# Hyena transform tables: split once, kept in a slab of their own for both layers

## Chip, cores and metric

One core of one Trainium2 chip runs the whole program in one launch. The metric is the time of an execution on the device in microseconds (us), the median over several runs; lower is better.

## What is computed

The reference is one step of a model with two layers over two streams of tokens, 128 of a prompt and 256 of a sample, 384 together, each token 1024 wide and in float32. A layer normalises, runs three token mixers on one projection, merges them by gates, and ends in a convolutional feed-forward part:

```python
h = rms_norm(x, lp["norm1"]) * (1 + sc1) + sh1
proj = h @ lp["w_in"]
q_a, k_a, v_a, cq, ckv, kpe, hy_in, gates = jnp.split(proj, _split_points(), axis=-1)
...
o_c = hyena_branch(hy_in, lp)
...
x = x + g1 * o
h = rms_norm(x, lp["norm2"]) * (1 + sc2) + sh2
x = x + g2 * conv_ffn(h, lp)
```

The third mixer, Hyena, filters 512 channels twice with long convolutions:

```python
u = dwconv3(hy_in, lp["hy_short_w"], lp["hy_short_b"])
v, x1, x2 = jnp.split(u, 3, axis=-1)
z = v
for n, gate in enumerate((x1, x2)):
    z = gate * (long_conv(z, kf[:, n]) + lp["hy_bias"][n] * z)
```

where `long_conv` is a product of Fourier transforms. The kernel does these transforms as matmuls with cosine and sine tables.

## The kernel before

Everything is feature-major: x lies in SBUF as 8 tiles of 128 features by 384 tokens. Products are kept at float32 accuracy by splitting both sides into a rounded part (hi) and the rest (lo) and adding three one-pass matmuls, hi by hi (line 267), hi by lo (line 268) and lo by hi (line 269), in `mm3`. A split is `hi_lo`: ScalarE rounds a copy (`copy_a`, line 229) and VectorE subtracts (line 233). Weights come by DMA from the queue of SyncE (SP) into a ring of two places (`load_w`, line 247; the modulation weights by line 368), are split, and wait in four pairs of places.

A layer begins with `norm_h`: a sum of squares by matmul (line 421), its root (line 403), a broadcast by matmul (line 427), and then for each of the 8 tiles a product on VectorE (line 236 through `tt`), scale and shift on ScalarE (line 435, two instructions for the two streams), and the split into hi and lo, which the even tiles have from VectorE alone (line 442 and line 236) and the odd ones from both engines (lines 229 and 233). The first product of `hyena_in` needs hi of a tile for lines 267 and 269 and lo for line 268. It runs through the 8 tiles for each block of 128 output features; three blocks can be under way, in three banks of PSUM.

The tables of the Hyena transforms are one input of 12 blocks of 128 by 128. `hyena_open`, called once in each layer between the two halves of `hyena_in`, takes memory for both parts from the arena FA, loads the input and splits it; `hyena_close` gives the memory back after the attention projections.

```python
def hyena_open(y):
    y.oT = [RA.alloc(4, T, top=True) for _ in range(2)]
    y.db = [RA.alloc(12, 128, top=True) for _ in range(2)]
    y.dt = [b.ap() for b in y.db]
    st = FA.alloc(12, 128)
    sp.dma_start(out=st.ap(), in_=t_dft.rearrange("p (a b) -> p a b", b=128))
    hi_lo(y.dt[0], y.dt[1], st.ap())
    st.free()
```

Their readers are the `mm3` calls of `hyena_chain`.

The order on each engine is not the order of the text: the framework schedules the whole program by a simulated time, so an instruction can stand far ahead of its place in the text once its inputs are there. In layer 1 the split of the tables, written after half of the projection, stands in the middle of the norm ahead of that projection. The engines take their instructions strictly in the order that was set.

Of the kernel before, what the change touches and what calls it, by code (L numbers as in the profile page):

```python
# [14 lines left out]
D = 1024  # L15
# [24 lines left out]
N_W = 4  # L40
N_BASE = 9728
SLABS = (1408, *[3072] * 9)
R_RE = 0.25
# [6 lines left out]
class Slab:  # L50
    """A place in SBUF, empty or a tile of one type; parts of it are given out."""

# [28 lines left out]
class Arena:  # L81
    """Memory given out by the order of emission: of the places that are free, the one free for longest."""

# [35 lines left out]
class Rounded:  # L119
    """The same memory, for parts that the tensor engine takes in one pass."""  # L120

# [38 lines left out]
class Ring:  # L160
    """Places of one size in turn."""

# [21 lines left out]
def kernel(  # L184
# [15 lines left out]
    split_slab = Slab(ctx, tc, 2 * N_W * 1024, "split")  # L200
    h_slab = Slab(ctx, tc, 2 * KD * T, "h")
    FA = Arena([Slab(ctx, tc, n, f"s{i}") for i, n in enumerate(SLABS)])
    RA = Rounded(FA)

    def banks(**lines):
        """Gives each line of work its banks of PSUM, which it takes in turn."""
        for line, own in lines.items():
            turns[line] = [int(b) for b in own]
# [12 lines left out]
    def ps_pair(line, n):  # L221
        """Two adjacent banks, the two parts of a tile in one each."""
        own = turns[line]
        b = min((b for b in own if b + 1 in own), key=lambda b: max(own.index(b), own.index(b + 1)))
        turns[line] = [q for q in own if q not in (b, b + 1)] + [b, b + 1]
        return all_banks[:, b:b + 2, 0:n]
# [4 lines left out]
    def hi_lo(hi, lo, src):  # L231
        copy_a(hi, src)
        dve.tensor_tensor(out=lo, in0=src, in1=f(hi), op=ALU.subtract)  # L233
# [68 lines left out]

# [1 line left out]
    def add_sq(k, src, first):  # L304
# [18 lines left out]

# [1 line left out]
    V_B, V_N1, V_N2, V_HW, V_HB, V_HF = 0, 48, 56, 64, 100, 112  # L325
# [45 lines left out]
    def mod_vec(l, v, ready=(), bufs=()):  # L371
        """One of the modulation vectors of both conditions; yields after each piece."""
        gv = ps_of("md", 512)
# [27 lines left out]
    def rstd_of(out, squares):  # L401
        """1 / sqrt(mean + eps) of the sums of squares of D elements."""
        act.activation(out=out, in_=squares, func=AF.Sqrt, scale=1.0 / D, bias=eps_t)
        dve.reciprocal(out=out, in_=out)

    def sqrt_ahead(part):
        """Has the activation engine load the function before the sums are complete."""
        b = FA.alloc(1)
        act.activation(out=b.ap(), in_=part, func=AF.Sqrt)
        b.free()  # L410

    def norm_h(l, which):
        """RMSNorm and modulation of x: the two f32r parts of h, feature-major."""
        hi, lo = h_parts
# [31 lines left out]
    def gemm_f(out, w, m):  # L446
        """The product of a block of weights; yields halfway through a long one."""
        kk = w[0].shape[1]
        for k in range(kk):
            mm3(out, at(w, slice(None), k), (m[0][:, k], m[1][:, k]), k == 0, k == kk - 1)  # L450
            if kk > 6 and k == 3:
                yield

    def conv3(l, dst, src, w0, w1, w2, bias):
        """Centred depthwise convolution of width 3 along the tokens of both streams."""
        act.activation(out=dst, in_=src, func=AF.Identity, scale=vec(l, w1), bias=vec(l, bias))  # L456
        for _, a, b in STREAMS:
            stt(dst[:, a + 1:b], src[:, a:b - 1], vec(l, w0), dst[:, a + 1:b], ALU.mult, ALU.add)
            stt(dst[:, a:b - 1], src[:, a + 1:b], vec(l, w2), dst[:, a:b - 1], ALU.mult, ALU.add)

# [1 line left out]
    def reduce_sin(l, dst, src, fr, b, n, np_):  # L462
        """sin(freq * (src + b)), the argument brought into [-pi, pi]."""
        a = FA.alloc(n)
# [14 lines left out]
    def filters(l, R, spec, first=False):  # L479
        """Spectra of the filters of a layer at the frequencies k + 1/2, per order (Re, Im) of the even and of the  # L480
        odd k for the sample's length, and (Re, Im) for the prompt's, each with the bias, a tap at 0; from the sums
        and differences of the two directions, where |f| + |b| = max(|f + b|, |f - b|) and the backward tap at 0 is
        left out; yields after each piece."""
        zt, w1, w2 = FA.alloc(T), FA.alloc(64), FA.alloc(2, 64)
# [173 lines left out]

# [1 line left out]
    C_E, C_O, I_E, I_O, C_P, I_P = 0, 2, 4, 6, 8, 10  # L660
# [4 lines left out]
    def hyena_start(l, spec):  # L665
# [5 lines left out]
        return y, line  # L671

    def hyena_open(y):
        y.oT = [RA.alloc(4, T, top=True) for _ in range(2)]
        y.db = [RA.alloc(12, 128, top=True) for _ in range(2)]
        y.dt = [b.ap() for b in y.db]
        st = FA.alloc(12, 128)
        sp.dma_start(out=st.ap(), in_=t_dft.rearrange("p (a b) -> p a b", b=128))
        hi_lo(y.dt[0], y.dt[1], st.ap())
        st.free()  # L680

    def hyena_close(y):
        for b in y.db:
            b.free()

    def hyena_in(y, hf, hT):
        """Projection and short convolution of half of the channels; token-major, the second half of the
        sample reversed."""
        l = y.l
# [34 lines left out]
    def hyena_chain(y, hf):  # L724
        """Both long convolutions of half of the channels and their gates."""
        R, dt, tok = RA, y.dt, y.tok[hf]
# [78 lines left out]

# [1 line left out]
    def attn_proj(l, hT, proj):  # L807
        """Queries, keys, values and latents, token-major, into (q k, v, cq ckv kpe) of each token tile."""
        col = 0
# [23 lines left out]
    def rope(dst, src, tab, i, heads, rd, tmp):  # L833
        """Rotates interleaved pairs: dst = src * cos + swapped(src) * (-sin, sin)."""
        cs = tab[:, i, 0].unsqueeze(1).to_broadcast([128, heads, rd])
        sn = tab[:, i, 1].rearrange("p (a b) -> p a b", b=2).unsqueeze(1).to_broadcast([128, heads, rd // 2, 2])
        sw = src.rearrange("p h (a b) -> p h a b", b=2)[:, :, :, ::-1]
        tt(tmp.rearrange("p h (a b) -> p h a b", b=2), sw, sn, ALU.mult)
        tt(dst, src, cs, ALU.mult)
        tt(dst, dst, tmp, ALU.add)  # L840

    def prep(l, proj, q, R):
        """Norms and rotations: queries, keys and latents, transposed."""
        gb = FA.alloc(768)
# [93 lines left out]
    def softmax(ps, nh, nk, scale):  # L938
        """Softmax over the last axis of the scores in PSUM."""
        pb = FA.alloc(nh, nk)  # L940
# [18 lines left out]
    def attention(heads, q_of, kp_of, ks_of, vp_of, vs_of, scale, oT, pairs=False):  # L959
        """Attention of a group of heads; the output feature-major."""  # L960
        jobs = []
# [3 lines left out]
        def scores(hs, i, n):  # L965
            """Queries by the one part of the keys, or by their two."""
            if pairs:
# [42 lines left out]
        def prompt_turn(hs, pb):  # L1010
            """Heads in order of parity in the tile."""
            for half in range(2):
# [58 lines left out]
    def mla(l, q, proj, oT, R):  # L1071
# [26 lines left out]
        def turned(qb, dst, sl):  # L1098
            """An even head is (nope, pe, 0) of 128 rows, an odd one (0, pe, nope)."""
            pt = ps_of("at", 4, 128)  # L1100
# [90 lines left out]
    def gates(l, n, hT, ring, out):  # L1191
        """tanh(g / 2) of the gate columns of a branch: sigmoid(g) is half of 1 + that."""
        for q in range(4):
# [12 lines left out]
    def branch(l, n, gs, oT, m, merged):  # L1206
        """Adds 2 * sigmoid(gates) * projection of a branch; the last halves the sum and splits it."""
        for q in range(4):
# [131 lines left out]
    class Ahead:  # L1340
        """Modulation vectors whose weights are loaded ahead, to fill the wait for a norm."""

# [22 lines left out]
    def urgent(line, by):  # L1365
        """The steps of a line, scheduled as if emitted that many instructions earlier."""
        if by < 0:
# [13 lines left out]
    def weave(main, *sides):  # L1381
        """Emits main with steps of the sides, (line, steps for each step of main), in between."""
        credit = [0.0] * len(sides)
# [11 lines left out]
    def mix(*lines):  # L1395
        """Steps of the lines in turn."""
        lines = list(lines)
# [58 lines left out]
    for l in range(NL):  # L1456
# [16 lines left out]
        finish(ch)  # L1473
        hyena_close(y)
        banks(**PS_AT)
# [139 lines left out]
```

## Time and profile before

| what | value |
|---|---|
| median of 3 runs | 1530.9 us (1530.8 to 1531.94) |
| span of the profiled execution, first to last instruction | 1528.9 us |
| median less span: what lies around the span | 2.0 us |
| TensorE busy (PE) | 1484.3 us, 97% |
| VectorE busy (DVE) | 1014.6 us, 66% |
| ScalarE busy (ACT) | 756.9 us, 50% |
| GpSimd busy (POOL) | 91.1 us, 6% |
| mean granted TensorE clock | 0.991 of full speed |

Busy time is the time in which an engine had an instruction under way. The table is to be read from TensorE down: the span holds 44.6 us in which TensorE had nothing under way, and a mean clock below 1 says that part of its busy time ran at the lower of its two clocks. All times below are counted from the first instruction of the span.

### The profile page before, as it was taken

The page shows a single profiled execution, that of the slowest core. Times are in us where ns is not written, and L with a number is a line of the kernel's source. Part 1 is how long each engine was busy: PE and PEld are TensorE (multiplying, and loading weights), DVE is VectorE, ACT ScalarE, POOL GpSimd, SP SyncE. Part 2 cuts the span into 40 slices and gives each one's busy share as a digit, 9 for nine tenths or more (in the row PEclk, how much of TensorE's full clock was granted, in tenths as well). Part 3 has the DMA queues.
Part 4 walks back from the last instruction along what each step waited for, and adds up shares of the span by engine and source line. Part 5 has one row for each costly group of instructions (what it writes and reads, how often), then busy time and mean ns, then how long its engine had stood idle before and what let it go on. Part 6 is the DMA issues. An engine that isn't in the chain of part 4 may idle for free.

```text
span 1528.9 us, 22323 instructions
## 1 busy us (share of the span) xinstructions
PE 1484.3 (97%) x8615; PEld 1349.2 (88%) x8615; DVE 1014.6 (66%) x1946; ACT 756.9 (50%) x1388; POOL 91.1 (6%) x120
## 2 busy tenths in 40 slices
PE   5999999999999999999999999999999999999997
PEld 2698799898779799999997988998887989999997
DVE  6868577455456796686776767874564767567674
ACT  3644365445454663453545444855454455344343
POOL 1113110000000000000000212000000000000000
PEclk9899999999999999999999999999999999999999
DMA  8634454334456533343265445242242424333531
GB/s 276 235 109 140 142 179 142 105 107 137 141 166 220 172 111 111 110 131 128 90 224 196 138 133 180 89 123 76 72 138 97 166 97 138 121 114 111 165 108 58
DMA packets 182448, 210.05 MB, mean 137 GB/s; under 512 B 25940, under 2 KB 166470, under 8 KB 182342
## 3 DMA queue, kind: packets, MB, share of 16 engines
q1 hardware_dynamic: 182342, 208.63, 42.2%
q8 instruction: 68, 1.11, 0.3%
q14 instruction: 38, 0.31, 0.1%
HBM read 206.48 MB, written 2.13 MB: 136 GB/s over the span
## 4 chain that ended last, share of the span: by engine, by line
PE 90%; DVE 3%; DMA 3%; ACT 2%; issue 1%; SPq 0%; DVEq 0%; ACTq 0%
PE banks L267 26%; PE banks L269 25%; PE banks L268 25%; PE banks L301 4%; PE banks L377 3%; PE banks L975 2%; PE banks L1003 2%; DVE s L236 1%; DMA base<-in_w_in_dram 1%; ACT s L229 1%; PE banks L605 1%; DMA s<-in_t_kdft_dram 1%; DVE split L233 1%; PE banks L550 1%; PE banks L991 0%
## 5 line engine op out<-in xcount | busy, mean ns | idle before, releaser
L229 ACT ACTIVATE split<-base 128x1024 fp32r<-128x1024 f32 (+2 forms) x272 | 280.1, 1040 | 347.6 <-PE banks L268 261.3
L233 DVE TENSOR_TENSOR split<-base,split 128x1024 fp32r<-128x1024 f32 (+2 forms) x272 | 328.5, 1214 | 168.4 <-ACT split L229 162.9
L267 PE MATMUL banks<-h,split 128*128 128x384 f32 x1280 | 435.9, 344 | 4.5 <-DVE h L442 2.5
L268 PE MATMUL banks<-h,split 128*128 128x384 f32 x1280 | 436.5, 341 | 0.6 <-DVE h L236 0.6
L269 PE MATMUL banks<-h,split 128*128 128x384 f32 x1280 | 432.6, 339 | 0.0
L267 PEld LDWEIGHTS banks<-h,split 128*128 128x128 f32 x1280 | 241.8, 189 | 20.3 <-issue 9.8
L268 PEld LDWEIGHTS banks<-h,split 128*128 128x128 f32 x1280 | 242.0, 189 | 5.6 <-issue 1.6
L269 PEld LDWEIGHTS banks<-h,split 128*128 128x128 f32 x1280 | 241.7, 189 | 2.8 <-issue 1.1
L268 PE MATMUL banks<-s,split 128*128 128x384 f32 x672 | 226.1, 337 | 0.0
L269 PE MATMUL banks<-s,split 128*128 128x384 f32 x672 | 225.0, 337 | 0.0
L267 PE MATMUL banks<-s,split 128*128 128x384 f32 x672 | 222.2, 340 | 1.0 <-ACT s L229 0.9
L229 ACT ACTIVATE s<-banks 128x384 f32<-128x384 f32 (+10 forms) x268 | 116.6, 464 | 155.0 <-PE banks L301 64.0
L239 DVE SCALAR_TENSOR_TENSOR s<-banks,base,s 128x127 f32<-128x127 f32 (+1 forms) x448 | 173.1, 410 | 10.2 <-ACT s L456 6.1
L267 PEld LDWEIGHTS banks<-s,split 128*128 128x128 f32 x672 | 125.5, 188 | 6.2 <-issue 2.3
L269 PEld LDWEIGHTS banks<-s,split 128*128 128x128 f32 x672 | 126.1, 188 | 3.3 <-DVE split L233 1.7
L229 ACT ACTIVATE s<-s 128x384 fp32r<-128x384 f32 (+4 forms) x142 | 81.9, 581 | 93.4 <-DVE s L236 47.1
L268 PEld LDWEIGHTS banks<-s,split 128*128 128x128 f32 x672 | 126.2, 188 | 0.5
L236 DVE TENSOR_TENSOR s<-banks,s 128x512 f32<-128x512 f32 (+3 forms) x132 | 81.5, 643 | 35.8 <-PE banks L269 17.3
L239 DVE SCALAR_TENSOR_TENSOR base<-banks,base 128x128 f32<-128x128 f32 (+1 forms) x128 | 46.9, 412 | 81.0 <-PE banks L269 81.0
L301 PE MATMUL banks<-base,s 128*128 128x128 f32 (+2 forms) x483 | 85.0, 276 | 5.6 <-DMA s<-in_hy_short_b_dram 4.2
L301 PEld LDWEIGHTS banks<-base,s 128*128 128x128 f32 (+2 forms) x483 | 60.1, 141 | 26.0 <-issue 9.7
L233 DVE TENSOR_TENSOR s<-s,s 128x512 fp32r<-128x512 f32 (+3 forms) x102 | 66.9, 658 | 20.8 <-ACT s L229 20.5
(151 smaller groups left out, 1741.1 us busy)
## 6 DMA issues: line engine op xcount, KB each, us to landing
base<-in_w_in_dram SPq DMA_DIRECT2D x40, 1024.0 KB
base<-in_ffn_up_dram SPq DMA_DIRECT2D x40, 1024.0 KB
base<-in_w_mod_dram SPq DMA_DIRECT2D x28, 1024.0 KB
s<-in_w_mod_dram SPq DMA_DIRECT2D x14, 1024.0 KB
base<-in_ffn_down_dram SPq DMA_DIRECT2D x16, 896.0 KB
base<-in_w_branch_dram SPq DMA_DIRECT2D x24, 512.0 KB
base<-in_w_out_dram SPq DMA_DIRECT2D x8, 1024.0 KB
base<-in_ffn_down_dram SPq DMA_DIRECT2D x8, 1024.0 KB
```

The costliest lines, as they stand in the source:

```text
L229: act.activation(out=out, in_=in_, func=AF.Copy, scale=scale)
L233: dve.tensor_tensor(out=lo, in0=src, in1=f(hi), op=ALU.subtract)
L236: dve.tensor_tensor(out=out, in0=a, in1=b, op=op)
L239: dve.scalar_tensor_tensor(out=out, in0=a, scalar=s, in1=b, op0=op0, op1=op1)
L267: pe.matmul(out, l[0], r[0], start=start, stop=False)
L268: pe.matmul(out, l[0], r[1], start=False, stop=False)
L269: pe.matmul(out, l[1], r[0], start=False, stop=stop)
L301: pe.transpose(out, in_, ident[:n, :n])
L377: pe.matmul(gv[32 * j:32 * j + 32], cT[:, 2 * k + j // 2], raw[:, j // 2, (j % 2) * 512:(j % 2) * 512 + 512], start=k == 0, stop=k == KD / ...
L550: pe.matmul(p.rearrange("p a b -> p (a b)"), hp[q].ap()[:, sl], ws.ap(), start=q == 0, stop=q == 1)
L975: pe.matmul(out, q_of(h)[:, i * 128:(i + 1) * 128], k, start=m == 0, stop=m == len(ks) - 1)
L1003: pe.matmul(po[b:b + 64], vs_of(h, n), pTs[h].ap()[:, n], start=n == 0, stop=n == 2, tile_position=(0, b))
```

## The change

The two parts of the tables get a slab of SBUF of their own, which is never given back. Only the first call of `hyena_open` loads and splits, in three pieces of four blocks each, which pass one after the other through staging memory; the second layer uses what is there. `hyena_close` goes. The scratch space for descriptors of software DMA is set to 2048 bytes of each partition. Docstrings and some comments are removed too, with no effect on the program but for line numbers (at first 2 higher, later 5).

```diff
+N_DFT = 12 * 128
...
     h_slab = Slab(ctx, tc, 2 * KD * T, "h")
+    dft_slab = Slab(ctx, tc, 2 * N_DFT, "dft")
     FA = Arena([Slab(ctx, tc, n, f"s{i}") for i, n in enumerate(SLABS)])
...
+    dft = []
+
     def hyena_open(y):
+
         y.oT = [RA.alloc(4, T, top=True) for _ in range(2)]
-        y.db = [RA.alloc(12, 128, top=True) for _ in range(2)]
-        y.dt = [b.ap() for b in y.db]
-        st = FA.alloc(12, 128)
-        sp.dma_start(out=st.ap(), in_=t_dft.rearrange("p (a b) -> p a b", b=128))
-        hi_lo(y.dt[0], y.dt[1], st.ap())
-        st.free()
-
-    def hyena_close(y):
-        for b in y.db:
-            b.free()
+        y.dt = dft
+        if dft:
+            return
+        dft.extend(b.ap(12, 128) for b in dft_slab.whole(F32R).cut(N_DFT))
+        tv = t_dft.rearrange("p (a b) -> p a b", b=128)
+        for a, b in ((8, 12), (0, 4), (4, 8)):
+            st = FA.alloc(b - a, 128)
+            sp.dma_start(out=st.ap(), in_=tv[:, a:b])
+            hi_lo(dft[0][:, a:b], dft[1][:, a:b], st.ap())
+            st.free()
...
         finish(ch)
-        hyena_close(y)
         banks(**PS_AT)
...
-    nc = _bacc.Bacc("TRN2", target_bir_lowering=False, num_devices=1)
+    nc = _bacc.Bacc("TRN2", target_bir_lowering=False, num_devices=1, dynamic_dma_scratch_size=2048)
```

Three places show how the engines' orders move. Names beginning with `s` are places of the arena, `h` the parts of the normalised tokens, `split` the split weights, `base` the long-lived memory, `banks` PSUM, `dft` the new slab; the numbers tell places apart and differ between the two programs.

VectorE in the norm at the start of layer 1, before, from the first four products to the third lo part (a row that writes `h` from `h`):

```order
L236 TENSOR_TENSOR s_3_1604<-base_98,banks 128x384 x4
L233 TENSOR_TENSOR s_4_6710<-s_6_6231,s_4_6710 128x1536
L442 CAST h_418<-s_3_1604 128x384
L236 TENSOR_TENSOR s_3_1604<-base_98,banks 128x384 x2
L442 CAST h_418<-s_3_1604 128x384
L236 TENSOR_TENSOR s_3_1604<-base_98,banks 128x384
L236 TENSOR_TENSOR h_418<-s_3_1604,h_418 128x384
L236 TENSOR_TENSOR s_3_1604<-base_98,banks 128x384
L233 TENSOR_TENSOR h_418<-s_3_1604,h_418 128x384 x2
```

and now:

```order
L238 TENSOR_TENSOR s_3_1609<-base_101,banks 128x384 x4
L444 CAST h_421<-s_3_1609 128x384
L238 TENSOR_TENSOR s_3_1609<-base_101,banks 128x384
L238 TENSOR_TENSOR h_421<-s_3_1609,h_421 128x384
L238 TENSOR_TENSOR s_3_1609<-base_101,banks 128x384
L444 CAST h_421<-s_3_1609 128x384
L238 TENSOR_TENSOR s_3_1609<-base_101,banks 128x384
L238 TENSOR_TENSOR h_421<-s_3_1609,h_421 128x384
L238 TENSOR_TENSOR s_3_1609<-base_101,banks 128x384
L235 TENSOR_TENSOR h_421<-s_3_1609,h_421 128x384
```

The subtraction over 1536 columns (line 233) is gone, and the lo part of the first tile stands second behind its CAST, where it stood fifth. On ScalarE the copy over 1536 columns ahead of the first scale and shift is gone too, and the rows around it are unmoved.

TensorE at the same place, before, from the broadcast to the matmuls on the first two tiles:

```order
L427 MATMUL banks<-s_5_6289,base_98 128x384
L377 MATMUL banks<-base_98 32x512 x8
L267 MATMUL banks<-h_418,split_417 128x384 x3
L268 MATMUL banks<-h_418,split_417 128x384
L269 MATMUL banks<-h_418,split_417 128x384
L267 MATMUL banks<-h_418,split_417 128x384
L268 MATMUL banks<-h_418,split_417 128x384
L269 MATMUL banks<-h_418,split_417 128x384
L267 MATMUL banks<-h_418,split_417 128x384
```

and now:

```order
L429 MATMUL banks<-s_5_5176,base_101 128x384
L379 MATMUL banks<-base_101 32x512 x8
L269 MATMUL banks<-h_421,split_420 128x384 x3
L270 MATMUL banks<-h_421,split_420 128x384
L271 MATMUL banks<-h_421,split_420 128x384
L270 MATMUL banks<-h_421,split_420 128x384
L271 MATMUL banks<-h_421,split_420 128x384
L270 MATMUL banks<-h_421,split_420 128x384
L271 MATMUL banks<-h_421,split_420 128x384
L269 MATMUL banks<-h_421,split_420 128x384 x3
```

All nine matmuls of the first tile, for three blocks of outputs, now stand ahead of those of the second tile (the last row); before, the two single rows of line 267 were already on the second tile.

ScalarE at the end of the norm of layer 0, now; before, the same rows stood there without the two that write `dft`, and the one copy of 128x1536 stood 17 rows behind the last row shown:

```order
L570 ACTIVATE s_1_124<-s_1_113 128x512
L437 ACTIVATE s_1_108<-s_1_108,base_101 128x128
L437 ACTIVATE s_1_108<-s_1_108,base_101 128x256
L231 ACTIVATE dft_769<-s_1_149 128x512
L231 ACTIVATE h_421<-s_1_108 128x384
L231 ACTIVATE s_1_113<-banks 128x512
L231 ACTIVATE h_421<-s_1_108 128x384
L231 ACTIVATE dft_769<-s_1_149 128x512
L231 ACTIVATE split_420<-base_101 128x1024
```

The second copy stands ahead of the last two hi parts of that norm (the rows that write `h`, of the sixth and the eighth tile), the third ahead of the next split of a weight; the first, not shown, stands 14 rows ahead of the second, behind the hi part of the second tile. The three subtractions on VectorE lie likewise. On SP the first piece's load stands where the one load stood; the other two stand one load further on, each waiting for the subtraction of the piece ahead of it, whose staging place it takes. Behind them stand, now, two loads of modulation weights and then the eleven small loads of layer 1's vectors (`load_vecs`), in two groups ahead of the next two weight blocks of the projection; before, those small loads stood behind five more blocks.

## Rows read from the trace of the kernel before

**Rows 1.** The page: span, and each engine's busy us, share of the span, instructions.

```profile
span 1528.9 us, 22323 instructions
PE 1484.3 (97%) x8615; PEld 1349.2 (88%) x8615; DVE 1014.6 (66%) x1946; ACT 756.9 (50%) x1388; POOL 91.1 (6%) x120
```

**Rows 2.** Stretches: length, busy of PE, PEld, DVE, ACT, POOL, granted clock, DMA share, GB/s.

```profile
80.00:340.00 260.00, 259.92 (x1544) 229.47 (x1543) 172.72 (x296) 132.38 (x255) 33.08 (x45) 1.00 0.43 136
820.00:840.00 20.00, 16.47 (x81) 12.38 (x81) 12.37 (x28) 12.31 (x24) 0.00 (x0) 0.83 0.65 214
840.00:1060.00 220.00, 220.00 (x1309) 202.22 (x1308) 154.13 (x260) 115.42 (x221) 30.51 (x41) 1.00 0.39 123
```

**Rows 3.** Stretches of 2 us in layer 1's norm, columns as in rows 2.

```profile
824.00:826.00 2.00, 0.52 (x8) 0.19 (x8) 2.00 (x3) 2.00 (x6) 0.00 (x0) 1.00 0.84 248
830.00:832.00 2.00, 2.00 (x8) 2.00 (x8) 0.95 (x4) 2.00 (x6) 0.00 (x0) 0.50 0.49 195
```

**Rows 4.** The chain of waits in layer 1's norm: start, us, engine, tile, line.

```profile
827.04 0.27 DVE h L442
827.77 0.48 DVE h L236
828.30 0.69 PE banks L268
829.31 0.32 PE banks L267
```

**Rows 5.** DVE by time, layer 1's norm: start, us, instruction, xcount, [idle before <-releaser].

```profile
822.23 1.95 DVE L236 TENSOR_TENSOR s<-base,banks 128x384 f32<-128x384 f32 x4 [0.72 <-PE banks L427]
824.10 1.75 DVE L233 TENSOR_TENSOR s<-s,s 128x1536 fp32r<-128x1536 f32 x1
```

**Rows 6.** ACT by time, the same stretch.

```profile
821.13 1.48 ACT L229 ACTIVATE s<-s 128x1536 fp32r<-128x1536 f32 x1 [0.82 <-DMA s<-in_t_dft_dram]
822.82 3.61 ACT L435 ACTIVATE s<-s,base 128x128 f32<-128x128 f32 x8 [0.21 <-DVE s L236]
826.34 0.92 ACT L229 ACTIVATE h<-s 128x384 fp32r<-128x384 f32 x2
```

**Rows 7.** PE by time, the same stretch and on to 844 us.

```profile
825.48 1.07 PE L377 MATMUL banks<-base 128*32 128x512 f32 x8 [2.29 <-DMA base<-in_w_mod_dram]
834.95 0.45 PE L268 MATMUL banks<-h,split 128*128 128x384 f32 x1
843.91 0.38 PE L301 MATMUL banks<-base,s 128*128 128x128 f32 x2
```

**Rows 8.** SP by time: two DMA issues ahead of that norm.

```profile
816.75 0.34 SPq L678 DMA_DIRECT2D s<-in_t_dft_dram  x1
817.95 0.37 SPq L368 DMA_DIRECT2D base<-in_w_mod_dram  x1
```

**Rows 9.** ACT by time, layer 0.

```profile
74.73 0.51 ACT L229 ACTIVATE h<-s 128x384 fp32r<-128x384 f32 x1
79.96 1.06 ACT L229 ACTIVATE split<-base 128x1024 fp32r<-128x1024 f32 x1 [4.72 <-PE banks L268]
105.89 1.49 ACT L229 ACTIVATE s<-s 128x1536 fp32r<-128x1536 f32 x1 [2.78 <-POOL s L613]
```

**Rows 10.** PE by time, layer 0, first matmuls on the sixth and eighth tile.

```profile
77.60 0.51 PE L267 MATMUL banks<-h,split 128*128 128x384 f32 x2
79.42 0.33 PE L267 MATMUL banks<-h,split 128*128 128x384 f32 x1
```

**Rows 11.** Groups by form: xcount, busy us, mean ns, idle before (DVE, then ACT).

```profile
L233 DVE TENSOR_TENSOR s<-s,s 128x512 fp32r<-128x512 f32 x44 | 33.1, 753 | 7.7 <-ACT s L229 7.4
L229 ACT ACTIVATE s<-s 128x512 fp32r<-128x512 f32 x52 | 32.5, 625 | 40.1 <-POOL s L761 24.2 <-DVE s L236 10.5 <-PE banks L269 2.4
```

**Rows 12.** Another stretch with an idle PE, columns as in rows 2.

```profile
1093.00:1096.40 3.40, 1.29 (x11) 1.01 (x9) 2.04 (x6) 3.05 (x4) 0.00 (x0) 1.00 0.00 0
```

**Rows 13.** The chain in layer 0's feed-forward part: a table of 320 KB lands.

```profile
516.36 2.65 DMA s<-in_t_kdft_dram
```

## The prediction

> **What bounds the kernel now.** I read the page first: TensorE (PE) is busy 97% of the span, VectorE (DVE) 66%, ScalarE (ACT) 50% [rows 1]. So time can come only from where PE waits or runs at its lower clock. The busy time by stretches says where that is. From 80 to 340 us, which holds layer 0's Hyena work and the old copy of the tables, PE has nothing to give back, and from 840 to 1060 us, layer 1's Hyena work, it is busy throughout. Between them, in the 20 us of layer 1's first norm, it is busy 16.47 us, and the granted clock is 0.83 on average [rows 2]. The finer stretches show the two levels: idle first (0.52 us busy of 2), then busy at 0.50, which is 1.2 of 2.4 GHz [rows 3]. Of these 20 us 3.5 us go to idle time and 0.17 x 20 = 3.4 us to the clock: 6.9 us is all that this place can return.
>
> The chain of waits there, and the timelines of DVE, ACT and PE, say why. TensorE's first matmul of the second pass (line 268) needs the lo part of the first tile, which ends at 827.77 + 0.48 = 828.25, and it starts at 828.30 [rows 4]. In front of that part DVE does the subtraction of the tables, 1.75 us from 824.10, straight behind the four products [rows 5]. ACT's copy of the tables ends at 822.6, and the scale and shift that follows waits for DVE anyway [rows 6]. PE also waits until 825.48 for a block of modulation weights [rows 7], which SP issued at 817.95, 1.2 us behind the load of the tables [rows 8].
>
> **The change, part by part.** *Layer 1's norm.* One load of 768 KB, one copy and one subtraction go, and the new order has nothing in their place. I rebuild the stretch with the durations of this trace, from the four products, which stay where they are.
>
> DVE: a product is 1.95 / 4 = 0.49 us [rows 5], a CAST 0.27, a lo part 0.48 [rows 4]. By the new order the first CAST ends at 824.10 + 0.27 = 824.37, a product at 824.86, the first lo part at 825.34: 2.9 us earlier than 828.25. Then product, CAST, product, lo, product and the lo part of the second tile: 0.49 + 0.27 + 0.49 + 0.48 + 0.49 + 0.48 = 2.70, so 828.04.
>
> ACT: eight scale and shifts from 822.82 to 826.43 [rows 6], unmoved. The hi part of the second tile follows alone: half of 0.92, so 826.89, ahead of its lo part on DVE. The other tiles then come from ACT faster than PE uses them.
>
> PE: the matmuls on modulation weights, twice 1.07 us [rows 7] from about 822.2, end near 824.3 if the second block has landed. Alone, that block needs no more than its share of the 1792 KB which both loads moved from 816.75 to 825.48: 1024/1792 x 8.7 = 5.0 us, so 822.9. The other bound is that it lands no earlier than now, at 825.48; I take 822.9, since the load ahead of it in the queue is gone. The nine matmuls of the first tile then run at 824.4 and 825.4 to 826.4, three of the second tile at 826.9, and from 828.04 PE has no more waits. Of the 72 matmuls for three blocks and 8 tiles 60 are left, and one more group on modulation weights. The pace is that of now: the 51 matmuls from 834.95 to 843.91 take 8.96 us, 0.176 each [rows 7]. So 828.04 + 60 x 0.176 + 1.07 = 839.7, against 843.91, where before the three blocks end: **4.2 us earlier**. If the block of modulation weights lands at 825.48, its matmuls end at 826.5, the nine of the first tile at 828.1 and the three next at 828.7, so 0.6 us more is lost: 3.6 us. In the best case the 2.7 us of this stretch that stay lost shrink further, up to the 6.9 us above.
>
> *What becomes of it.* From there PE is busy 220.00 of 220 us [rows 2]: what starts earlier ends earlier. No wait stands behind it that a clock time sets; loads wait for places that PE and DVE free, and come earlier with them.
>
> *Layer 0's norm.* ACT gets three copies of 512 columns at 0.63 us and DVE three subtractions at 0.75 us [rows 11]. The two copies ahead of the last hi part delay it by 1.25 us, from 75.2 to 76.5 [rows 9]; with two subtractions, 1.5 us, in front of its lo part on DVE, 78.0 at worst. The first matmul on the eighth tile runs at 79.42; that on the sixth, whose hi part is ready before the eighth's, at 77.60 [rows 10]. So PE, which has older matmuls queued, covers it: 0. Without this cover it would be 2.8 us, the lot, and the range takes a part of it. The third copy stands ahead of a weight split at 79.96 which ACT began only after 4.72 us of waiting for PE [rows 9]. Its load waits for the second subtraction, at about 76; a table of 320 KB took 2.65 us to land [rows 13], so 256 KB is there by 79: 0.
>
> *Layer 0, the rest.* The old copy at 105.89 goes, with 2.78 us of idle time ahead of it on ACT [rows 9] and PE busy throughout [rows 2]: 0. On SP the eleven small loads now stand ahead of two weight blocks; at 0.37 us an issue [rows 8] that is 4.1 us. Splits wait in four pairs, so three blocks of 24 matmuls are ready, 72 x 0.176 = 12.7 us of cover: 0. The memory given back and the scratch space cost nothing: all loads are SP's. Elsewhere the orders differ little; I allow 0.8 us either way.
>
> **Sum:** -4.2 us on the profiled span of 1528.9 us. The median lies 2.0 us above that span; 1530.9 - 4.2 = **1526.7 us**.
>
> **The rivals.** *The clock falls all the same.* TensorE still meets waits of 0.5 us between bursts. Before, the low clock covered 0.17 x 20 x 2 = 6.8 us, at 0.32 us a matmul for 0.17 [rows 4]. If it begins as now, near 826.7, and lasts to 833.5, 5.5 us of the new full stretch run at half pace: 2.7 us lost, gain 1.5. If it lasts half as long, 1.0 to 1.7 us are lost, gain 2.5 to 3.2. That is 1527.7 to 1529.4. For it: this norm fell. Against it: nine matmuls more lie ahead of 826.7, and from 1093.0 to 1096.4 PE was busy 1.29 us of 3.4 with the clock at 1.00 throughout [rows 12]. [...] Chance 0.24.
>
> *Handed back.* PE reaches a later wait earlier and stays there: a load or DVE sets the pace. It would show as PE idle after 840 us, of which there is none in the next 220 us [rows 2]. 1530.9 us, chance 0.10.
>
> *Slower: layer 0's weights come late.* SP now waits twice for a subtraction and once for the last reader of the small loads' place, with weight blocks queued behind. If that holds a block up for longer than the 12.7 us of split weights, PE stands still from 80 us on, and every further us is lost. It decides from 12.7 + 4.2 = 16.9 us of delay; the issues alone make 4.1. At 20 us it gives 1530.9 - 4.2 + 7.3 = 1534.0. Chance 0.08.
>
> That the change doesn't do what it says is out: the new order has no copy or subtraction of tables in layer 1.
>
> **How the numbers follow.** The forecast has the remaining 0.58. The range runs from 1.5 us below it, part of what the ceiling leaves, to 1530.2, the clock's worst case with 0.8 us for the order: 1525.2 to 1530.2. It leaves out the slower rival, most of the handing back and a larger gain. A measurement of this kernel can tell about 0.2%, 3.1 us, from no change. Faster by more than that, below 1527.8, is the forecast but for its upper edge, and the mildest fall of the clock: 0.61. Slower by more, above 1534.0: 0.07. Within: 0.32.
>
> **What would show it.** In the profile after, the stretch from 820 to 840 us has less than 3 us of idle PE and a clock of 1.00; the first matmul of line 270 on `h` starts 2.9 us earlier against the four products; no DVE row of 1536 columns; stretches before 820 us as they are. A clock of 0.83 there means the first rival, new idle time between 80 and 340 us the third, and idle time after 840 us the second. The forecast is wrong if the same norm ends less than 3 us earlier in the span.

## The result and the profile after

The changed kernel takes 1548.3 us (median of 4 runs, 1547.26 to 1550.03) where the kernel before took 1531.1 in the same comparison: ratio 1.011, interval 1.0097 to 1.0122. It is 17 us slower. The forecast was 1526.7 us, and its range ended at 1530.2: the sign was wrong. The profiled execution has a span of 1546.8 us, 17.9 more than before.

The page after, span and first section, against [rows 1]:

```profile
span 1546.8 us, 22301 instructions
PE 1493.6 (97%) x8615; PEld 1352.9 (87%) x8615; DVE 1014.8 (66%) x1947; ACT 756.0 (49%) x1389; POOL 90.7 (6%) x120
```

The 8615 records of TensorE are the same in number. PE is busy 9.3 us longer with the same matmuls, and idle 8.6 us longer. So there are two kinds of loss, and only one shows as a wait. Of the 9.3 us, 3.1 are matmuls on modulation weights (below), and up to 3.4 are a lower clock: behind the first 100 us it stood at half for 17.0 us, against 10.2 before. The rest is not assigned. To find the places, I took the start of TensorE's n-th instruction in both traces. The comparison is exact where both have taken the same matmuls up to that point, as they have in each of these rows:

| point in TensorE's order | before, us | after, us | after is later by |
|---|---|---|---|
| 201st: layer 0, ahead of the norm's matmuls | 57.46 | 58.34 | 0.9 |
| 1905th: layer 0, in the attention | 352.90 | 368.13 | 15.2 |
| 4611th: the broadcast in layer 1's norm | 821.28 | 837.00 | 15.7 |
| 4701st: layer 1, three blocks nearly done | 842.52 | 854.12 | 11.6 |
| 5097th: layer 1, further on | 908.33 | 923.02 | 14.7 |
| last | 1519.39 | 1537.22 | 17.8 |

The loss comes in layer 0, where I had put down nothing. In layer 1 the norm does return 4.1 us, and 3.1 of them are gone by the 5097th instruction. The last 3.1 us come behind it, with two falls of the clock: from 1111.3 to 1114.7 us, where it stayed up before, and from 1254.7 to 1261.5, where before it was low from 1239.6 to 1243.0. banks_before (below), which has the order of before up to both places, shows the same two falls (1097.0 to 1100.4 and 1240.4 to 1247.2), so nothing ties them to the change. The stretches of the changed kernel show the losses of both layers (columns as in [rows 2]):

```profile
80.00:340.00 260.00, 253.45 (x1462) 220.43 (x1460) 161.73 (x278) 124.98 (x238) 32.94 (x42) 0.99 0.43 133
224.00:231.00 7.00, 3.03 (x19) 1.72 (x18) 6.07 (x10) 5.09 (x11) 4.69 (x5) 0.98 0.55 176
329.00:339.00 10.00, 7.59 (x48) 5.27 (x48) 5.78 (x10) 6.72 (x18) 0.00 (x0) 1.00 0.49 151
836.00:856.00 20.00, 18.12 (x101) 13.15 (x99) 12.06 (x29) 12.05 (x26) 0.00 (x0) 1.00 0.59 199
854.00:860.00 6.00, 3.72 (x17) 3.10 (x16) 5.98 (x12) 3.40 (x5) 0.29 (x1) 0.89 0.50 154
```

From 80 to 340 us, where PE was busy 259.92 of 260 [rows 2], it is now idle 6.5 us, 4.0 of them at 224 to 231 and 2.4 at 329 to 339. The norm of layer 1 (836 to 856, the place of 820 to 840 in [rows 2]) now has 18.12 us of busy PE and a clock of 1.00. But behind it, from 854 to 860, 2.3 us are idle and the clock falls.

**Layer 0: one wait of 22 us on VectorE.** The timeline of DVE before has the two products of one step of the Hyena chain, `tt(m1, ...)` and `tt(m2, ...)`, in one row:

```profile
146.58 1.27 DVE L236 TENSOR_TENSOR s<-banks,s 128x512 f32<-128x512 f32 x2
```

and in the changed kernel:

```profile
151.57 0.68 DVE L238 TENSOR_TENSOR s<-banks,s 128x512 f32<-128x512 f32 x1
...
162.70 0.16 DVE L344 COPY base<-banks 128x4 f32<-128x4 f32 x1 [2.75 <-PE banks L303]
...
168.58 0.27 DVE L353 COPY base<-banks 128x112 f32<-128x112 f32 x1
...
174.34 0.34 DVE L361 COPY base<-banks 128x176 f32<-128x176 f32 x1 [5.49 <-PE banks L303]
174.59 0.68 DVE L238 TENSOR_TENSOR s<-banks,s 128x512 f32<-128x512 f32 x1
```

The first and the last row are the same two products. Here the second comes 23.0 us after the first, right behind the last of three copies of `load_vecs` (lines 344, 353, 361). In the compiled program the second product writes columns 0 to 511 of arena slab `s0`, the place that `load_vecs(1)` has its four rows of staging in, and it waits on two of their DMAs. The arena goes by the order of the text: there this place had been given back, while on the chip it was in use until 174.3 us. The changed requests for memory had shifted who gets which place.

The chain is then late for the work that was to stand beside it. The chain of waits at the first stall says so, and TensorE's timeline has the three waits:

```profile
224.47 0.69 DVE s L238
...
225.23 2.33 POOL s L766 x2
...
227.59 0.63 ACT s L231
...
228.23 1.28 ACT L1207
...
229.53 0.50 ACT s L1207
```

```profile
225.71 1.07 PE L379 MATMUL banks<-base 128*32 128x512 f32 x8 [1.18 <-DMA base<-in_w_mod_dram]
228.27 0.50 PE L269 MATMUL banks<-s,dft 128*128 128x256 f32 x2 [1.49 <-ACT s L231]
230.07 0.45 PE L269 MATMUL banks<-h,split 128*128 128x384 f32 x1 [1.30 <-ACT s L1207]
```

The first 1.2 us of the idle time go to a load of modulation weights. Then come the steps of the Hyena chain (line 766, then its split), for whose products PE has to stand because the order has nothing else ahead of them, and then a load of a function table for the gates (line 1207). Before, the same step on GpSimd (there line 761) began at 202.56 us instead of 225.23. The clock falls behind these waits, from 230.7 to 234.1 us: 3.4 us at half pace, 1.7 lost.

```profile
230.70:234.10 3.40, 3.40 (x12) 3.40 (x12) 0.69 (x1) 0.71 (x2) 0.00 (x0) 0.50 0.02 2
```

**Layer 0: the same matmuls, in more pieces.** This is the part in which PE is busy. A step on modulation weights is four matmuls of 32 columns side by side, eight records. One step in the kernel before:

```profile
90.99 1.07 PE L377 MATMUL banks<-base 128*32 128x512 f32 x8
91.99 0.33 PE L301 MATMUL banks<-base,s 128*128 128x128 f32 x1
```

and half a step in the changed kernel:

```profile
97.89 1.05 PE L379 MATMUL banks<-base 128*32 128x512 f32 x4
98.88 0.48 PE L607 MATMUL banks<-s,s 128*128 128x256 f32 x1
```

From its start to the next instruction eight records take 1.00 us, and four take 0.99. The other half is paid again at 101.7 us. The orders have 57 such pieces before and 60 now; between 60 us and TensorE's 2419th instruction (444.89 us before, 461.92 now) it is 21 and 26.

**Layer 1: the norm returns its 4 us, and the next block takes them.** TensorE by time, changed kernel:

```profile
855.34 0.34 PE L271 MATMUL banks<-h,split 128*128 128x384 f32 x1
856.89 0.45 PE L269 MATMUL banks<-h,split 128*128 128x384 f32 x1 [1.21 <-ACT split L231]
857.17 0.34 PE L270 MATMUL banks<-h,split 128*128 128x384 f32 x1
857.35 0.27 PE L303 MATMUL banks<-base,s 128*128 128x128 f32 x1
858.68 0.68 PE L271 MATMUL banks<-h,split 128*128 128x384 f32 x1 [1.07 <-DVE split L235]
```

The three blocks end at 855.5, and PE waits 1.21 us for the hi part of the next block's weights and 1.07 for their lo part. In the compiled program this block reads the third of the four places for split weights, which is free only when the third block has ended. The fourth place had been split at 831 us, but the block that uses it needs the first block's bank of PSUM. Before, the blocks ended one after the other (three blocks, some 2.9 us apart), and bank and split came in time. Now they end within 3 us, and another block, of the second half, is put ahead. That it is put there because the bank isn't free when the framework's simulated time asks for it is argued from the order; the runs with four banks test it.

### The profile page after: what moved, and what is told of

Read it like the earlier page. It is cut to its first block, busy times and chain, and to the rows that moved or that the text cites. A ratio compares the mean times of both kernels' runs of the same rounds, so it can differ in the third digit from the quotient of the medians.

```text
span 1546.8 us, 22301 instructions
## 1 busy us (share of the span) xinstructions
PE 1493.6 (97%) x8615; PEld 1352.9 (87%) x8615; DVE 1014.8 (66%) x1947; ACT 756.0 (49%) x1389; POOL 90.7 (6%) x120
## 4 chain that ended last, share of the span: by engine, by line
PE 89%; DVE 4%; DMA 3%; ACT 2%; issue 1%; SPq 1%; POOL 0%; DVEq 0%; ACTq 0%
PE banks L269 25%; PE banks L270 25%; PE banks L271 25%; PE banks L303 3%; PE banks L379 3%; PE banks L980 2%; PE banks L1008 2%; DVE split L235 1%; DVE s L238 1%; PE banks L607 1%; ACT s L231 1%; DMA s<-in_t_kdft_dram 1%; DMA base<-in_w_branch_dram 1%; PE banks L552 1%; ACT split L231 1%
## 5 line engine op out<-in xcount | busy, mean ns | idle before, releaser
L231 ACT ACTIVATE s<-banks 128x384 f32<-128x384 f32 (+9 forms) x268 | 117.9, 465 | 164.5 <-PE banks L303 59.0
L238 DVE TENSOR_TENSOR s<-banks,s 128x512 f32<-128x512 f32 (+3 forms) x132 | 81.6, 645 | 40.7 <-PE banks L271 15.2
L303 PE MATMUL banks<-base,s 128*128 128x128 f32 (+1 forms) x483 | 83.5, 276 | 6.7 <-DMA s<-in_hy_short_b_dram 3.8
L303 PEld LDWEIGHTS banks<-base,s 128*128 128x128 f32 (+1 forms) x483 | 59.4, 141 | 27.4 <-issue 10.1
L458 ACT ACTIVATE s<-banks,base 128x384 f32<-128x384 f32 x112 | 73.4, 655 | 15.2 <-PE banks L271 15.2
```

The lines of the kernel that those rows point to most:

```text
L231: act.activation(out=out, in_=in_, func=AF.Copy, scale=scale)
L238: dve.tensor_tensor(out=out, in0=a, in1=b, op=op)
L303: pe.transpose(out, in_, ident[:n, :n])
```

## The experiments

Theory A: two orders, one in each layer, lose what the change brings, by a place in memory and by a bank. Theory B: the added work itself (copies, subtractions, loads) costs it. Theory D came with the rows above: a cut step costs 1 us a piece.

**The staging place.** `vecs_later`:

```diff
-        if l == 0:
-            finish(vl[1])
         weave(attn_proj(l, hT, proj), (md, R_MD), (ch, R_CH))
+        if l == 0:
+            finish(vl[1])
```

> The changed kernel, but the last pieces of layer 1's vectors (load_vecs) are emitted behind the attention projection instead of ahead of it, so that their staging place is not given to the Hyena chain's products while their loads are under way. Theory A (the Hyena chain of layer 0 stands 22 us for that place, and what PE lacks later is its cover): the idle 4.0 us and the low clock (1.7 us) at 224 to 231 us and the 2.4 us at 329 to 338 us go, 8.1 us together, so about 1540 us; if the rest of layer 0's loss hangs on the same order, down to 1533. TensorE reaches layer 1's first broadcast at 821 to 829 us of the span, against 836.3. Theory B (the three pieces themselves, or loads that SP issues late): no change, 1547 to 1549 us.

Measured: 1540.5 us, ratio to before 1.006 (1.0045 to 1.0075): 7.8 us less than the changed kernel, where A had 8.1. The pair of products in its trace:

```profile
151.14 1.27 DVE L238 TENSOR_TENSOR s<-banks,s 128x512 f32<-128x512 f32 x2
```

Two products in one go, and PE is busy 82.00 of 82 us from 150 to 232. The broadcast of layer 1 is reached at 829.6, just behind the 821 to 829 that were expected. The three pieces and the loads are as in the changed kernel, so B is out for these 8 us. The rest of layer 0's loss stayed.

**One piece.** `one_piece`:

```diff
-        for a, b in ((8, 12), (0, 4), (4, 8)):
+        for a, b in ((0, 12),):
```

> The changed kernel, but the tables come in one piece of 12 blocks into the slab in layer 0, still only once. In its order layer 0's second half of the Hyena chain stands behind 711 matmuls instead of 817. Theory A (a place in the arena that the chain waits for; the pieces only moved who gets which place): 1533 to 1540 us, within 3 us of the kernel with the later vectors. Theory B (the three copies and subtractions in the norm cost the time): also faster, but the kernel with the later vectors stays at 1548. Theory C (any early split of the tables disturbs layer 0): both stay at 1546 to 1549 us.

Measured: 1539.95 us, ratio 1.0056 (1.0041 to 1.0071). It doesn't touch `load_vecs`, and in its compiled program the second product lies beside the first in another slab; the pair is together at 151.17 us, in 1.27 us as above. Theories B and C, which kept one or both of these kernels at 1546 us or more, are out. The kernel with the later vectors keeps the three pieces and this one keeps `load_vecs` where it was, and both lose the pause: so neither costs it by itself; what costs it is that the two met.

**Only the slab and the scratch space.** `slab_only` is the kernel before with

```diff
+    Slab(ctx, tc, 3072, "dft").whole(F32)
     FA = Arena([Slab(ctx, tc, n, f"s{i}") for i, n in enumerate(SLABS)])
...
-num_devices=1)
+num_devices=1, dynamic_dma_scratch_size=2048)
```

> The kernel before, with the scratch space of 2048 bytes and a slab of 3072 columns that is taken and never used, so that the arena lies at the changed kernel's addresses; every order is that of before. Theory A: no difference, 1530 to 1532 us. Rival (the place in SBUF or the smaller scratch space costs time, for instance by conflicts of engines at an address): slower by 2 us or more, up to the 17 us of the change.

Measured: 1531.38 us, ratio 1.0001 (0.9991 to 1.001). No cost. Its trace holds a second lesson. The orders are those of before, and so is the norm of layer 1, with the subtraction in it, but here the clock didn't fall:

```profile
822.00:842.00 20.00, 15.92 (x93) 12.11 (x93) 14.82 (x32) 13.67 (x25) 0.48 (x1) 1.00 0.64 210
```

PE is idle 4.1 us of 20, more than in [rows 2], at a clock of 1.00 where that was 0.83. The same orders and the same waits, and the clock falls in one execution and not in the other. The kernel before varies by itself, too: in the comparison that holds layer1_only, 5 of its 27 runs have a mean granted clock of 0.994 or more, and the others 0.989 to 0.992.

**Four banks.** `four_banks`, the changed kernel with

```diff
-        banks(**PS_HY0)
+        banks(**(PS_HY0 if l == 0 else {**PS_HY0, "mm": "0123", "fl": "5"}))
```

> The changed kernel, but layer 1's first half of the projection has four banks of PSUM for its blocks instead of three. Theory A for layer 1 (the norm does end 4 us earlier, and TensorE then stands on a block whose weights are not split, because the block whose weights are ready has no bank): the 2.3 us of idle time at 855 to 859 us and the 1.7 us of low clock behind it go, so 4 us less than the changed kernel, 1544.3 us, and up to 2 us more if the fourth block fills the norm. Theory B (what the norm gives is lost to a load or to DVE behind it, whatever the banks): 1547 to 1549 us. Layer 0 is the same order and should show the same stalls.

Measured: 1547.1 us, 1.2 us less where 4 were expected: inconclusive by the total. Its profile has a longer low clock in layer 0, 6.8 us at 228 us for 3.4, and two more of 3.4 us at 368 and 546, which have nothing to do with layer 1. In layer 1 the stall is gone. `vecs_banks` has both edits:

> The changed kernel with both earlier edits: the last pieces of layer 1's vectors behind the attention projection, and four banks for the first half of layer 1's projection. Theory A (two separate losses, each from an order): the 7.8 us that the later vectors gave and the 2.3 us of idle time with up to 1.7 us of low clock that four banks took away add up: 1548.3 - 7.8 - 2.3 to 4.0 = 1536.5 to 1538.2 us. Rival (one loss seen at two places, the second only moves): 1540 us, as with the later vectors alone.

Measured: 1536.9 us, ratio 1.0039 (1.0027 to 1.0051), within what A gave. The two losses add up: 7.8 and 3.6 us, each with some 2 us of noise.

**Layer 1 by itself.** `layer1_only` is the kernel before, with nothing changed in layer 0:

```diff
+    dft_slab = Slab(ctx, tc, 3072, "dft")
...
-        y.db = [RA.alloc(12, 128, top=True) for _ in range(2)]
-        y.dt = [b.ap() for b in y.db]
+        y.db = [RA.alloc(12, 128, top=True) for _ in range(2)] if y.l == 0 else dft_slab.whole(F32R).cut(1536)
+        y.dt = [b.ap(12, 128) for b in y.db]
...
-num_devices=1)
+num_devices=1, dynamic_dma_scratch_size=2048)
```

> The kernel before, with layer 0 as it is, word for word in every order; only layer 1's tables go to a slab of their own instead of the arena, so that their load and split (still made) stand in the feed-forward part ahead of the norm. Layer 1's norm then has the changed kernel's order: half of the change by itself. The prediction's theory (what the norm gives is kept): 1531.2 - 4.2 = 1527 us. Theory A for layer 1 (TensorE then stands 2.3 us on a block whose weights are not split, and its clock may fall): the stretch from the broadcast on is 4 us shorter up to the end of three blocks and then gives it back: 1529.5 to 1531.5 us, with idle time 15 to 20 us behind the broadcast.

Measured: 1531.9 us, ratio 1.0003 (0.9994 to 1.0012): nothing gained, 5 us above the prediction's theory and 0.4 above the upper end of A. TensorE by time:

```profile
842.23 0.44 PE L268 MATMUL banks<-h,split 128*128 128x384 f32 x1 [1.21 <-ACT split L230]
842.51 0.34 PE L269 MATMUL banks<-h,split 128*128 128x384 f32 x1
842.68 0.27 PE L302 MATMUL banks<-base,s 128*128 128x128 f32 x1
844.03 0.44 PE L270 MATMUL banks<-h,split 128*128 128x384 f32 x1 [1.07 <-DVE split L234]
```

The same two waits, to the hundredth, as in the changed kernel; behind them the clock falls here too, from 844.8 to 848.2 us. `layer1_four_banks` adds the line of banks:

> As layer1_only, with four banks for the first half of layer 1's projection. Theory A: the block whose weights are ready has a bank, so the stall behind the three blocks is gone and what the norm gives is kept: 1531.2 - 3.5 = 1527.7 us, between 1526.5 and 1529, faster than both kernels. Rival (banks don't matter, the loss comes from loads or DVE): as layer1_only.

Measured: 1528.6 us, ratio 0.998 (0.9971 to 0.9989): the only version faster than both, by 0.2%. Behind its norm PE has no wait:

```profile
820.00:840.00 20.00, 18.67 (x102) 12.94 (x99) 9.95 (x27) 10.00 (x23) 0.00 (x0) 1.00 0.49 159
840.00:860.00 20.00, 20.00 (x119) 17.50 (x119) 14.38 (x31) 10.90 (x18) 2.65 (x5) 1.00 0.67 211
```

The control, `banks_before`, has the line of banks alone, with the split still in the norm:

> The control: the kernel before with the four banks alone, the tables' split still in the middle of layer 1's norm. If the four banks were all of the gain, as fast as layer1_four_banks (1527.7 us). By theory A the split still holds up the first lo part, by 2.9 us, which a fourth block covers only in part: 1529 to 1531 us.

Measured: 1531.4 us, ratio 0.9995 (0.9986 to 1.0004). Four banks alone give nothing; split and banks have to go together.

The time from the broadcast (4611th instruction of TensorE) to the 5097th, up to which all these profiles have taken the same matmuls, sorts them (us):

| order of layer 1's norm | clock falls in it or just behind | does not fall |
|---|---|---|
| split in the norm (before, slab_only) | 87.1 | 84.9 |
| split in the norm, four banks (banks_before) | 86.9 | |
| no split in the norm (after, vecs_later, layer1_only; one_piece) | 86.0, 86.1, 86.0 | 84.5 |
| no split, four banks (four_banks, vecs_banks, layer1_four_banks) | | 83.5, 83.5, 83.5 |

At the same clock the removed split is worth 0.4 us (84.9 to 84.5) with three banks and 1.4 us with four. The rest of what layer1_four_banks gained is a clock that stayed up in all three profiles of that order. The runs agree: 9 of its 11 have a mean granted clock of 0.994 or more, and the kernel before has 5 of 27; the medians of these are 1528.3 and 1530.2 us, 1.9 apart where all runs are 3.0 apart.

**Pieces of a step.** To keep the four matmuls together I put them into a section that the scheduler doesn't break (below): on the kernel before (`whole_groups_before`), on the changed one (`whole_groups_after`), and with the two other edits (`whole_groups_all`).

```diff
-            for j in range(4):
-                pe.matmul(
+            with tc.tile_critical():
+                for j in range(4):
+                    pe.matmul(
...
```

> The kernel before, with the four matmuls of a step on modulation weights kept together in the order (a section that the scheduler doesn't break). Theory D (a step costs 1.0 us on TensorE however many of its four matmuls stand together, so each cut costs 1.0 us more; the traces show 8 records in 1.00 us and 2, 4 or 6 records in 0.98): the order of before has 57 such pieces, this one 48, so 9 x 0.98 = 8.8 us less, 1522 us, with 3 us either way for the rest of the order. Rival (the time of a cut piece is only shown there, since TensorE would wait anyway): no change, 1531 us.

> The changed kernel with the same edit. Its order has 48 pieces instead of 60, and the second half of layer 0's Hyena chain stands behind 703 matmuls instead of 817, so the pause should be gone without any edit to the vectors. Theory D with theory A: 1548.3 - 12 x 0.98 - 8.1 = 1528 us, or less. Against the kernel before with the same edit, whose order in layer 1's norm is the same, it tells what the tables' second load and split cost by themselves: by the prediction's sum 4.2 us; if the norm's gain hung on the order alone, 0 to 1 us, so the same time as that kernel.

> The changed kernel with whole groups, the later vectors and four banks. By the sum of the three separate effects: 1548.3 - 11.8 - 8.1 - 2.3 to 4.0 = 1524 to 1526 us, faster than both kernels. If the order with whole groups has already taken away the pause and the stall, no better than the changed kernel with whole groups alone.

Measured: 1778.8, 1785.1 and 1771.8 us, ratios 1.161, 1.166 and 1.156. A miss of 250 us that says nothing for or against D: such a section makes TensorE stand still in front of it. From the list of waits in `whole_groups_before`, the wait of TensorE's weight loads for these steps (us in total, times, longest):

```profile
PEld banks L378 <- issue: 167.5, 48, 14.0
```

48 sections, 3.5 us of waiting each, and the mean granted clock fell to 0.927. What the tables' second load costs on otherwise equal orders can't be read from these three either. `cut_groups` went the other way, the kernel before with more cuts:

```diff
-            for j in range(4):
-                pe.matmul(
+            with tc.high_priority(offset=20):
+                for j in range(4):
+                    pe.matmul(
...
```

> The kernel before with the matmuls on modulation weights at a higher priority, which cuts their groups of four into more pieces: 87 instead of 57 in the order. Theory D (each piece costs TensorE 1.0 us whether one, two, three or four matmuls stand together): 30 x 0.98 = 29 us more, 1560 us, with 5 us either way for the rest of the order; the matmuls on modulation weights take 85 to 92 us instead of 60.5. Rival (what a cut piece shows is waiting that another instruction would take otherwise): 1531 to 1538 us.

Measured: 1578.5 us, one run, 47 us more, beyond the 29 and its 5. TensorE's records on modulation weights alone, over the whole span, of before, of the changed kernel and of `cut_groups` (busy PE first):

```profile
0.00:1600.00 1600.00, 60.42 (x384) 10.20 (x384) 0.99 0.41 131
```

```profile
0.00:1600.00 1600.00, 63.52 (x384) 10.61 (x384) 0.99 0.41 131
```

```profile
0.00:1600.00 1600.00, 94.71 (x384) 13.66 (x384) 0.99 0.41 131
```

The same 384 records take 34.3 us longer. The order has 90 pieces of a step, 33 more than before (the expectation's 87 counts short where a stretch runs over the end of a step), so 1.04 us each. A single matmul takes as long as four:

```profile
116.07 1.04 PE L378 MATMUL banks<-base 128*32 128x512 f32 x2
117.05 0.33 PE L301 MATMUL banks<-base,s 128*128 128x128 f32 x1
```

So D holds for the pieces themselves; the remaining 13 us are of the rest of that order and weren't followed up. In layer 0 the changed kernel pays the pieces too. From 60 us to TensorE's 2419th instruction, up to which both have taken the same matmuls, first before, then after (PE busy on modulation weights first):

```profile
60.00:445.00 385.00, 23.12 (x128) 3.22 (x128) 0.99 0.43 137
```

```profile
60.00:462.00 402.00, 28.30 (x128) 3.87 (x128) 0.98 0.43 132
```

28.30 - 23.12 = 5.2 us for 5 more pieces, in which PE counts as busy. Beyond that instruction the new order has two pieces fewer (34 for 36), so over the span 3.1 us are left.

## Why the prediction was wrong, step by step

*The rebuilding of layer 1's norm* was right to a tenth. Shifted by the 15.72 us that the changed kernel is late, it gave 841.06 us for the first lo part, 843.76 for that of the second tile, and 855.4 for the end of the three blocks. The chain of waits has

```profile
840.63 0.47 DVE h L238
...
843.23 0.48 DVE h L235
...
843.75 0.44 PE banks L270
```

thus 841.10 and 843.71, and the blocks end at 855.34 + 0.17 = 855.51. The clock stayed at 1.00 in the norm, as forecast.

*"From there PE is busy 220.00 of 220 us: what starts earlier ends earlier"* failed. That row was of the old order, in which the blocks end one by one. I had the new order in front of me and followed it to the end of the three blocks, not to the one behind them. There it stands on a split that its own predecessors hold up: 2.3 us idle and 3.4 us at half pace, 4.0 together, against the 4.1 gained. This is the second rival, handed back, which I gave 0.10 and looked for in a load or on DVE; it was a place for split weights and a bank. layer1_only shows it alone.

*The size of the gain* rested on one execution in which the clock fell. 2.2 of the 4.2 us were that fall (87.1 against 84.9), and slab_only shows the same order without it. I asked whether the clock would still fall after the change, and not whether it always falls before. Behind the three blocks the clock fell after waits of 1.21 and 1.07 us in after and layer1_only, and stayed up after nearly the same in one_piece:

```profile
851.45 0.44 PE L269 MATMUL banks<-h,split 128*128 128x384 f32 x1 [1.38 <-ACT split L231]
853.08 0.45 PE L271 MATMUL banks<-h,split 128*128 128x384 f32 x1 [0.90 <-DVE split L235]
```

The Trainium skill (TensorE: Matmul & The Clock Gate, section HAM oscillation) tells of a kernel in which waits for loads, longer than the bursts of matmuls between them, throttle the engine each time. No run shows that pattern at this place; behind waits as short as these the clock fell in some executions and not in others, in the old order as in the new.

*"Layer 0, the rest: 0 ... Elsewhere the orders differ little; I allow 0.8 us either way"* is the step that cost the sign: 15.2 us by the 1905th instruction. 0.9 was there ahead of the norm and isn't of the change: slab_only, with the orders of before, has 0.8 at the same instruction. vecs_later, without the wait for the staging place, is at the 1905th at 358.15 us, 10.0 us ahead of the changed kernel (7.8 by the medians of the whole). The 5.2 us that it is still behind the kernel before hold 3.1 us of cut steps and 0.5 from ahead of the norm; some 1.7 us are not assigned. The matmuls on modulation weights up to that instruction, for before, after and vecs_later:

```profile
60.00:352.90 292.90, 15.74 (x96) 2.20 (x96) 0.98 0.42 132
```

```profile
60.00:368.13 308.13, 19.89 (x96) 2.72 (x96) 0.98 0.41 127
```

```profile
60.00:358.15 298.15, 18.85 (x96) 2.58 (x96) 0.98 0.42 131
```

With the edit to the vectors and four banks the kernel still stands 8.3 us above layer1_four_banks (1536.9 against 1528.6), which has the same order in layer 1. Half of it is cut steps (27.27 us on modulation weights up to the 2419th instruction, 4.2 more than in layer1_four_banks). The other half stays open: its profile has two falls of the clock that the other's doesn't have, from 358.0 to 361.4 and from 535.5 to 538.9 us, 1.7 us each, and no run shows whether the order or chance brings them. No run undoes the cut steps alone, either.

*Layer 0's norm, the copies and subtractions in it: 0* was about right: the lag grows from 0.9 to 1.1 us over it (313th instruction, 83.83 us before), and to 1.3 in slab_only, which has the old order. *The slab and the scratch space: 0* was right (slab_only). *The slower rival*, weights late by SP, had the sign at 0.07 and the wrong cause: of the small loads that moved I counted the issues and not the place that they land in, which was the one thing of them that mattered.

## What to carry to other kernels

Where a scheduler and an arena decide order and addresses, an edit that frees work on one engine can move the whole program. So count the rows that move, follow each moved chain to the next thing it needs (a place, a bank, a slot for weights), and treat "the orders differ elsewhere" as a cost of unknown sign, not as zero. A norm that ends earlier is worth only what the block behind it can take; give it a bank and split weights in the same edit. And before a fall of the clock goes into a sum, look at a second execution of the same program.

## What the runs showed of the hardware

Four matmuls of 32 columns that stand together take 1.00 us on TensorE, and one, two or three of them alone 0.97 to 0.99; 90 pieces for 57 cost 34.3 us of busy TensorE (cut_groups). The Trainium skill (TensorE: Matmul & The Clock Gate, Part 3: Packing small matmuls) says that matmuls on separate groups of columns run at the same time; the records agree, and show what is lost when something stands between them. The granted clock fell in layer 1's norm in one execution of an order (before, 3.5 us of idle PE in 20) and not in another (slab_only, 4.1 us). And a section that the scheduler must not break cost TensorE 3.5 us of waiting at each of its 48 places (whole_groups_before).
